# Attention units in a queue with wider distances, unnormalized head probabilities, gate b ahead of merge a, and no weight prefetch into the opening

## The chip, the cores and the metric

The kernel runs on one core of a Trainium2 chip. The metric is device time in microseconds, the median of several executions. One execution was also recorded by the hardware profiler; all views of the profile in this document are of that execution.

A core has TensorE (PE, matrix products from SBUF into PSUM), VectorE (DVE), ScalarE (ACT), GpSimd (POOL) and SyncE (SP, which here issues nearly all DMAs). Each engine works through its own list of instructions in order and waits on semaphores for the others.

## The reference

Two layers of a bidirectional encoder over 512 tokens with 1024 channels, in float32:

```
for i in range(DEPTH):                                   # 2
    h = rmsnorm(x, norm_mix[i])
    qa, ka, va, glu_in, qc, kc, vc, gates = split(h @ w_in[i])
    ya = diff_attention(qa, ka, va, ...)                 # 4 heads of two softmaxes
    yb = conformer_conv(glu_in, ...)                     # GLU, 31 taps, layernorm, silu
    yc = neighbourhood_attention(qc, kc, vc, rpb[i])     # 8 heads, 8x16 windows
    ga, gb, gc = split(sigmoid(gates))
    x = x + (ga * (ya @ w_br_a[i]) + gb * (yb @ w_br_b[i]) + gc * (yc @ w_br_c[i])) @ w_o[i]
    h = rmsnorm(x, norm_ffn[i])
    x = x + (silu(h @ w_ffn_gate[i]) * (h @ w_ffn_up[i])) @ w_ffn_down[i]
    h = rmsnorm(x, norm_ple[i])
    x = x + sigmoid(h @ w_ple_gate[i]) * (p[i] @ w_ple_in[i])
return rmsnorm(x, norm_final)
```

In differential attention a head has two softmaxes over 512 keys, and its output passes through an rmsnorm of its own:

```
a = softmax(s)                               # s: two score maps of a head
a = a[:, :, 0] - lam * a[:, :, 1]
o = rmsnorm(a @ v, subln_g) * (1 - lam_init)
```

## The kernel before

Activations lie channels by tokens: eight tiles of 128 x 512. Every float32 operand is split into a float32r high part (ACT copy, `split`, line 125) and a low part (DVE subtraction, line 139), and a product takes three matmuls: high x high, high x low, low x high (`mm3`, lines 159 to 161). A weight block of 128 x 1024 is loaded by SP into `wr` (512 KB) and split into `wh` and `wl` by `weights`; these instructions get a priority 400 instructions ahead of their place in the program (`w_ahead`).

The order on PE is the program's own. On the other engines and DMA queues a planner sets the order at compile time: among the instructions that it holds to be ready it takes the one with the highest priority, by its own estimates of durations.

A *tick* is four chunks of a projection; a chunk is the three matmuls of one 128-channel piece. At every tick the generators in `live` that are due take their next step, so that attention steps are placed between chunks of projections. A `yield n` in a generator means n ticks later. A unit is started by `run(gen, delay)`, with a delay in ticks after its head's projections.

A layer goes through these stages:
1. *glu*: eight projections, gated into `z`, the input of the convolution.
2. *natten*: four head pairs. `natten_in` projects Q and K, scales them, and `stack` builds by DMA the operands of `scores`, which hold high and low parts in the two halves of the partitions. Four units a pair: two score tiles of 128 x 256, exponential and normalization on ACT (`scale`), then transposes, then the product with V. Units start 3, 4, 5 and 6 ticks after the projections; the steps lie 2 and 1 ticks apart.
3. *diff*: four heads. `rope` copies a projection, lets DMA turn it, and combines both on DVE; then `stack`. Four units a head, one for each 128 queries (`probs`: two score maps, two maxima, two exponentials with their sums, the first map scaled by its reciprocal sum on ACT, the second subtracted on DVE), started 4, 6, 8 and 10 ticks after the projections. The odd units go on: transposes 2 ticks later, the product with V 1 tick later, and after the second half the head's norm: statistics 1 tick later, the broadcast of the result 2 ticks later.
4. *gate c* (eight projections, one of them among the heads), a sigmoid over all of them, *branch c*, *merge a* (per block a projection, a sigmoid and a product), *gate b* (eight projections), *merge b*, *w_o*, then *ffn* and *ple*.

The depthwise convolution is DVE work in the background: 4 x 31 taps (line 142, `conv_z`). `background` issues a given number of them (`BG`) behind a named instruction; `conv`, which is started at block 1 of gate b, issues what is left, sums the four results, and after two ticks PE forms the mean (`mu`, line 465, tile `conv_tr`).

PSUM has eight banks: `mm` 3 for projections, `sc` 2 for scores, `tr` 2 for transposes and norms, `av` 1.

`opening` loads x, the parameters and the first four weight blocks in pieces, and warms PE up with `WARM` matmuls on zeros. `final` does the last block of ple in two halves and the last norm.

Of the kernel before, what the change touches and what calls it, by code (L numbers as in the profile page):

```python
# [20 lines left out]
P = 128  # L21
# [26 lines left out]
WARM = 14  # L48
NORM = (1, 1)
BG = dict(glu=4, natten=3, gatec=2, branchc=2, mergea=4, mergea2=3)  # L50
# [8 lines left out]
class Net:  # L59
    def __init__(self, nc, tc, a):  # L60
        self.nc, self.tc, self.a = nc, tc, a
        self.uid = 0
        self.phase = "pre"
        self.act_set = None
        self.act_now = []
        self.act_prev = []
        self.live = []
        self.units = []
        self.wait = []
        self.now = 0  # L70
        self.chunks = 0
        self.col = self.rb = None

    def run(self, gen, delay=0):

        e = [self.now + delay, gen, self.phase]
        self.live.append(e)
        if not delay:
            self.step(e)
        return e  # L80
# [67 lines left out]
    def weights(self, ap, n):  # L148
        with self.tc.high_priority(offset=self.w_ahead):
            raw = self.sb("wr", [P, 1024])  # L150
            hi = self.sb("wh", [P, 1024], F32R)
            lo = self.sb("wl", [P, 1024], F32R)
            self.nc.sync.dma_start(raw[:, :n], ap[:, :n])
            self.split(hi[:, :n], lo[:, :n], raw[:, :n])
        return hi, lo
# [21 lines left out]
    def norm(self, sq, n, waits, done, spread=True):  # L177
# [10 lines left out]
        nc.vector.tensor_scalar(ms, sm, 1.0 / n, EPS, ALU.mult, ALU.add)  # L188
# [26 lines left out]
    def operand(self, x, g, tag):  # L215

        h = self.sb(tag, [P, 2, 512], F32R)
# [22 lines left out]
    def build(self):  # L240
        nc, tc, a = self.nc, self.tc, self.a
        self.bufs = dict(wr=2, wh=3, wl=3, h=8, qk=4, kh=2, v=4, pt=2, y=5, z=5, x=8, t=8, rp=4,
                         e=4, a=3, r=4, ss=1, sm=8, rc=4, b=4, s=8)
        self.bg, self.norm_on, self.w_ahead = BG, NORM, 400
# [12 lines left out]
    def opening(self):  # L257
# [5 lines left out]
        xc = [self.sb("x", [P, 512]) for _ in range(KD)]  # L263
# [7 lines left out]
        blocks = []  # L271
        for m in range(4):
            src = a["w_in"][0, (OFF_GLU + (0 if m % 2 else CB)) // P + m // 2]
            blocks.append((src, self.sb("y", [P, 1024], F32R), self.sb("qk", [P, 1024], F32R),
# [4 lines left out]
        for k in range(KD):  # L279
# [5 lines left out]
            if k in pieces:  # L285
                c0, c1, tag = pieces[k]
                for src, wh, wl, _ in blocks:
                    raw = self.sb(tag, [P, c1 - c0])
# [13 lines left out]
            self.tick()  # L302
        return h
# [51 lines left out]
    def layer(self, i, h, xsrc, xs):  # L355
# [14 lines left out]
        acc = []  # L370
# [83 lines left out]
    def conv(self, cs, ys):  # L454
# [16 lines left out]
        def done(col, rb):  # L471
            for j, c in enumerate(cs):
# [6 lines left out]
                y = self.sb("y", [P, 2, 512], F32R)  # L479
# [39 lines left out]
    def natten_in(self, pr, st, ys):  # L519
# [5 lines left out]
        qk = []  # L525
        for off in (OFF_QC, OFF_KC):
            ps = self.proj(off + pr * P)
            t = self.sb("t", [P, 512])
            r = self.rb if off == OFF_KC else st["r8"]
            self.background(self.tt(t, ps, r, ALU.mult), self.bg["natten"])  # L530
            qk.append(self.stack(t, off == OFF_KC))
        box = {}
        ys.append(self.sb("y", [P, 2, 512], F32R))
        for n in range(4):
            self.run(self.natten_unit(pr, n // 2, n % 2, *qk, st, box, ys[pr]), 3 + n)

    def natten_v(self, g, st):
# [6 lines left out]
        vd = [self.sb("x", [P, 2, 256], F32R) for _ in range(2)]  # L544
# [6 lines left out]
    def natten_unit(self, pr, half, u, q, k, st, box, y):  # L551
# [5 lines left out]
        for t in range(2):  # L557
            qt = 2 * half + t
            sc = self.ps("sc", (P, NW))
            self.scores(sc, q, k, u, slice(qt * P, (qt + 1) * P),  # L560
# [16 lines left out]
            self.scale(e[:, own], m[:, 2:3], self.norm_on[0])  # L577
# [25 lines left out]
        yield 1  # L603
# [18 lines left out]
    def gate_c(self, acc, m):  # L622
        self.phase = "gatec"
        ps = self.proj(OFF_G + 2 * D + m * P)
        g = self.sb("x", [P, 512])
        self.background(self.tt(g, ps, self.rb, ALU.mult), self.bg["gatec"])
        acc.append(g)
# [8 lines left out]
    def merge_a(self, ys, acc):  # L636
        for m in range(KD):
            self.phase = "mergea"
            ps = self.proj(OFF_G + m * P)
# [6 lines left out]
            self.background(self.tt(acc[m], acc[m], g, ALU.add), self.bg["mergea2"])  # L646

    def gate_b(self, cs, ys):
        gs = []
        for m in range(KD):  # L650
            self.phase = "gateb"
            if m == 1:
                conv = self.run(self.conv(cs, ys))
            ps = self.proj(OFF_G + D + m * P)
            if m % 2 == 0:
                two = self.sb("v", [P, 2, 512])
            g = two[:, m % 2]
            self.tt(g, ps, self.rb, ALU.mult)
            self.act(g, g, AF.Sigmoid, table="sigmoid")
            gs.append(g)  # L660
        self.drain(conv)
        return gs

    def merge_b(self, ys, acc, gs):
        self.phase = "mergeb"
        out = []
        for m in range(KD):
# [4 lines left out]
            mg = self.sb("qk" if m < 4 else "v", [P, 2, 512], F32R)  # L672
# [4 lines left out]
    def stack(self, t, key):  # L677

        nat = self.sb("kh", [P, 512], F32R)
        self.act(nat, t, AF.Copy)
        low = t.bitcast(F32R)
        self.tt(low, t, nat.bitcast(F32), ALU.subtract)
        sts = []
        for own, far in ((nat, low), (low, nat))[:2 if key else 1]:
            if own is low or not key:
                st = self.sb("qk", [P, 2, 512], F32R)
                st = [st[:, u] for u in range(2)]  # L690
            else:
                st = [self.sb("x", [P, 512], F32R) for u in range(2)]
            for u in range(2):
                rs, rx = slice(64 * u, 64 * u + 64), slice(64 - 64 * u, 128 - 64 * u)
                self.nc.sync.dma_start(st[u][rs].bitcast(F32), own[rs].bitcast(F32))
                self.nc.sync.dma_start(st[u][rx].bitcast(F32), far[rs].bitcast(F32))
            sts.append(st)
        return sts if key else st

    def scores(self, out, q, k, u, qs, ks):  # L700
        for n, st in enumerate(k):
            self.nc.tensor.matmul(out, q[u][:, qs], st[u][:, ks], start=n == 0, stop=n == 1)  # L702

    def rope(self, ps, cr, sr, key):
        raw = self.sb("rp", [P, 512])
        self.act(raw, ps, AF.Copy, scale=1.0 if key else 0.125)
        rot = self.sb("rp", [P, 512])
        for b in range(4):
            o = b ^ 1
            self.nc.sync.dma_start(rot[32 * b:32 * b + 32], raw[32 * o:32 * o + 32])  # L710
        self.tt(raw, raw, cr, ALU.mult)
        self.tt(rot, rot, sr, ALU.mult)
        self.tt(raw, raw, rot, ALU.add)
        return self.stack(raw, key)

    def diff_in(self, head, st, ys):
# [8 lines left out]
        q = self.rope(self.proj(OFF_QA + head * P), *st["tabs"], False)  # L725
        k = self.rope(self.proj(OFF_KA + head * P), *st["tabs"], True)
        box = {}
        for qt in range(4):
            self.run(self.diff_unit(head, qt, q, k, st, box, ys), 4 + 2 * qt)
# [5 lines left out]
    def diff_unit(self, head, qt, q, k, st, box, ys):  # L735
# [3 lines left out]
        box[qt] = self.probs(q, k, qt)  # L739
        if t == 0:  # L740
            return
        yield 2
# [12 lines left out]
        yield 1  # L755
# [9 lines left out]
        if half == 0:  # L765
            return
        o = self.sb("t", [P, 512])
# [10 lines left out]
        yield from self.norm(sq, P, (1, 2), done, spread=False)  # L778

    def scale(self, t, s, on_act):  # L780
        if on_act:
            self.act(t, t, AF.Copy, scale=s)
        else:
            self.nc.vector.tensor_scalar(t, t, s, None, ALU.mult)

    def probs(self, q, k, qt):
# [5 lines left out]
        for u in range(2):  # L792
            sc = self.ps("sc")
            self.scores(sc, q, k, u, qs, slice(0, 512))
# [3 lines left out]
                     accum_out=m[:, 2 + u:3 + u])  # L798
            es.append(e)
        nc.vector.reciprocal(m[:, 4:6], m[:, 2:4])  # L800
        nc.vector.tensor_scalar(m[:, 6:7], m[:, 5:6], self.nlam[:, i:i + 1], None, ALU.mult)
        self.scale(es[0], m[:, 4:5], self.norm_on[1])
        self.stt(es[0], es[1], m[:, 6:7], es[0], ALU.mult, ALU.add)
        return es[0]

    def w_o(self, mg, xsrc):
        self.phase = "wo"
        xs, h, st = [], [], []
        for m in range(KD):
            xo = self.sb("x", [P, 512])  # L810
# [9 lines left out]
    def ffn(self, h, x):  # L820
# [3 lines left out]
        for half in range(2):  # L824
# [23 lines left out]
            for m in range(KD):  # L848
# [3 lines left out]
                if half:  # L852
                    hn.append(self.norm_chunk(m, x[m], self.par(i, "ple", m),
                                              "qk" if m < 4 else "v", st))
# [49 lines left out]
    def final(self, h, x, pairs, hn, most):  # L904
# [50 lines left out]
        def store(c, col, tiles):  # L955
            r = self.sb("qk", [P, 1024])
# [3 lines left out]

        pg = [self.ps("mm", (P, 256)), None]
# [8 lines left out]
        rest(pi[0], 0)  # L970
        lows = [turn("av", 0, 0), turn("tr", 0, 1)]
# [119 lines left out]
```

## Time and profile before

| | |
|---|---|
| Time, median of 3 runs | 1901.37 us (1900.05 to 1901.43) |
| The profiled execution's own time | 1901.63 us |
| Its span, first to last instruction | 1899.8 us |
| Mean granted TensorE clock | 0.989 |
| PE busy | 1850.4 us (97%), 8912 matmuls |
| DVE busy | 1190.5 us (63%) |
| ACT busy | 769.3 us (40%) |
| POOL busy | 29.3 us (2%) |
| Moved by DMA | 213.82 MB, 113 GB/s in the mean |

Busy time is the time in which an engine had an instruction under way. [...] Waits are named by the instruction that waited and by the one whose end released it. The granted clock is 1.00 at full speed and 0.50 at half.

### The profile page before, as it was taken

The numbers are of one execution on the slowest core, as the hardware profiler recorded it, in microseconds if no ns is written. First come the engines' busy times: TensorE is split into PE (matmuls) and PEld (weight loads), VectorE is DVE, ScalarE is ACT, GpSimd is POOL, SyncE is SP. The second block draws the span as 40 slices with busy tenths as digits, with TensorE's granted clock in tenths as the row PEclk, the third lists the DMA queues.
The fourth block names the chain that finished last, engine by engine and source line by source line (L and its number), as shares of the span: only waits on it lengthen the run. The fifth ranks groups of instructions, "written<-read, shape, count | busy, mean of one in ns | idle before, by whom it ended". The sixth has DMA issues, their size and how long they took to land.

```text
span 1899.8 us, 23913 instructions
## 1 busy us (share of the span) xinstructions
PE 1850.4 (97%) x8912; PEld 1551.0 (82%) x8912; DVE 1190.5 (63%) x1921; ACT 769.3 (40%) x1296; POOL 29.3 (2%) x88
## 2 busy tenths in 40 slices
PE   8999989999999999999999998999999999999998
PEld 6898777887888888888888987788788888888887
DVE  6777677996654434445767767679876443344454
ACT  5466555224432222223525665443344322222343
POOL 0000000000000000000000000000000000000000
PEclk9999999999999999999999999999999999999999
DMA  5566432331432232222436654323233222322222
GB/s 181 157 171 178 123 105 57 105 111 61 161 105 95 85 104 103 97 84 92 143 121 176 177 142 133 89 62 100 94 117 133 95 100 79 110 100 93 88 89 86
DMA packets 89940, 213.82 MB, mean 113 GB/s; under 512 B 12256, under 2 KB 29792, under 8 KB 89824
## 3 DMA queue, kind: packets, MB, share of 16 engines
q1 hardware_dynamic: 89392, 211.60, 35.3%
q8 instruction: 71, 1.16, 0.3%
q10 hardware_dynamic: 432, 0.69, 0.1%
q14 instruction: 45, 0.37, 0.1%
HBM read 176.59 MB, written 4.19 MB: 95 GB/s over the span
## 4 chain that ended last, share of the span: by engine, by line
PE 87%; DVE 6%; DMA 3%; ACT 2%; SPq 1%; issue 1%; DVEq 0%; POOL 0%; POOLq 0%; ACTq 0%
PE ffn_mm L161 13%; PE ffn_mm L159 13%; PE ffn_mm L160 13%; PE mergea_mm L160 2%; PE mergea_mm L159 2%; PE mergea_mm L161 2%; PE wo_mm L159 2%; PE wo_mm L161 2%; PE wo_mm L160 2%; PE ple_mm L159 2%; PE ple_mm L160 2%; PE ple_mm L161 1%; PE natten_mm L159 1%; PE natten_mm L161 1%; PE natten_mm L160 1%; PE diff_mm L160 1%
## 5 line engine op out<-in xcount | busy, mean ns | idle before, releaser
L125 ACT ACTIVATE ffn_wh<-ffn_wr 128x1024 fp32r<-128x1024 f32 (+1 forms) x152 | 144.2, 949 | 511.6 <-issue 350.3
L159 PE MATMUL ffn_mm<-wo_h,ffn_wh 128*128 128x512 f32 x704 | 274.2, 390 | 0.0
L161 PE MATMUL ffn_mm<-wo_h,ffn_wl 128*128 128x512 f32 x704 | 273.9, 389 | 0.0
L160 PE MATMUL ffn_mm<-wo_h,ffn_wh 128*128 128x512 f32 x704 | 273.9, 389 | 0.0
L139 DVE TENSOR_TENSOR ffn_wl<-ffn_wr,ffn_wh 128x1024 fp32r<-128x1024 f32 (+1 forms) x152 | 164.9, 1085 | 129.3 <-ACT ffn_wh L125 129.3
L142 DVE SCALAR_TENSOR_TENSOR conv_z<-glu_z,pre_par,conv_z 128x512 f32<-128x512 f32 x240 | 179.1, 746 | 2.5
L161 PEld LDWEIGHTS ffn_mm<-wo_h,ffn_wl 128*128 128x128 f32 x704 | 132.2, 188 | 27.6
L160 PEld LDWEIGHTS ffn_mm<-wo_h,ffn_wh 128*128 128x128 f32 x704 | 132.2, 188 | 27.4
L159 PEld LDWEIGHTS ffn_mm<-wo_h,ffn_wh 128*128 128x128 f32 x704 | 132.2, 188 | 27.1
L139 DVE TENSOR_TENSOR ffn_t<-ffn_t,ffn_mm 128x512 f32<-128x512 f32 x44 | 30.2, 687 | 114.8 <-PE ffn_mm L161 114.8
L139 DVE TENSOR_TENSOR ffn_t<-ffn_mm,wo_r 128x512 f32<-128x512 f32 x44 | 30.4, 691 | 111.3 <-PE ffn_mm L161 111.3
L159 PE MATMUL ffn_mm<-ffn_z,ffn_wh 128*128 128x512 f32 x160 | 62.2, 389 | 0.0
L160 PE MATMUL ffn_mm<-ffn_z,ffn_wh 128*128 128x512 f32 x160 | 62.2, 389 | 0.0
L161 PE MATMUL ffn_mm<-ffn_z,ffn_wl 128*128 128x512 f32 x160 | 62.2, 389 | 0.0
L159 PE MATMUL ffn_mm<-ffn_y,ffn_wh 128*128 128x512 f32 x160 | 62.2, 389 | 0.0
L160 PE MATMUL ffn_mm<-ffn_y,ffn_wh 128*128 128x512 f32 x160 | 62.2, 389 | 0.0
L161 PE MATMUL ffn_mm<-ffn_y,ffn_wl 128*128 128x512 f32 x160 | 62.2, 389 | 0.0
L125 ACT ACTIVATE mergea_wh<-mergea_wr 128x1024 fp32r<-128x1024 f32 (+1 forms) x32 | 27.1, 848 | 82.8 <-PE mergea_mm L160 66.7
L795 DVE TENSOR_REDUCE diff_s<-diff_sc 128x1 f32<-128x512 f32 x64 | 42.3, 682 | 8.5 <-PE diff_sc L702 8.5
L125 ACT ACTIVATE natten_wh<-natten_wr 128x1024 fp32r<-128x1024 f32 x24 | 25.4, 1058 | 50.5 <-PE glu_mm L160 20.0
L139 DVE TENSOR_TENSOR wo_x<-wo_x,ffn_mm 128x512 f32<-128x512 f32 x32 | 22.0, 687 | 34.1 <-PE ffn_mm L161 34.1
L125 ACT ACTIVATE natten_e<-natten_b,natten_s 128x256 f32<-128x256 f32 x64 | 32.2, 503 | 27.1 <-DVE natten_s L565 25.8
(452 smaller groups left out, 4738.5 us busy)
## 6 DMA issues: line engine op xcount, KB each, us to landing
ffn_wr<-w_fg SPq DMA_DIRECT2D x44, 512.0 KB, 3.3
ffn_wr<-w_fu SPq DMA_DIRECT2D x44, 512.0 KB, 3.2
ffn_wr<-w_fd SPq DMA_DIRECT2D x32, 512.0 KB, 3.5
natten_wr<-w_in SPq DMA_DIRECT2D x16, 512.0 KB, 3.6
natten_b<-bias SPq DMA_DIRECT2D x64, 128.0 KB, 2.5
diff_wr<-w_in SPq DMA_DIRECT2D x16, 512.0 KB, 3.6
gatec_wr<-w_in SPq DMA_DIRECT2D x16, 512.0 KB, 3.7
mergea_wr<-w_in SPq DMA_DIRECT2D x16, 512.0 KB, 3.3
```

Of the source, the lines that this page charges most:

```text
L125: i = self.nc.scalar.activation(out, in_, func, **kw)
L139: return self.nc.vector.tensor_tensor(out, a, b, op)
L142: return self.nc.vector.scalar_tensor_tensor(out, a, s, b, op0, op1)
L159: mm(out, wh, ah, start=first, stop=False)
L160: mm(out, wh, al, start=False, stop=False)
L161: mm(out, wl, ah, start=False, stop=last)
L795: nc.vector.tensor_reduce(out=m[:, u:u + 1], in_=sc, op=ALU.max, axis=AX.X, negate=True)
```

## The change

- `opening`: `WARM` goes from 14 to 10. The priority of a weight block reaches back at most to the opening's end (`p0`), so no block of a later stage stands ahead of the opening's own loads. Its buffers are allocated in pairs.
- Units are put into a queue (`later`) with a delay and a gap: at each tick at most one unit starts, not before its delay is over and not before the gap behind the last one. natten: delay 5, gap 1; diff: delay 6, gap 2. The steps of a natten unit lie 2 and 2 ticks apart (2 and 1 before), those of a diff unit 3 and 2 (2 and 1 before).
- The first map of a diff head is left unnormalized. With s0 and s1 the sums of the exponentials e0 and e1, the unit forms e0 - lam (s0 / s1) e1, which is s0 times the row as it was. The head's norm takes the factor out, with its epsilon multiplied by s0 squared. ACT's copy of 128 x 512 per unit goes away.
- Gate b's first two blocks stand ahead of the sigmoids over gate c, its other six behind branch c and ahead of merge a. `conv` starts at block 4 of merge a. `BG` is set anew.
- Tiles of the tags `qk`, `x` and `v` are allocated as pairs of twice the size, half as many (`qk` 2 instead of 4, `x` 4 instead of 8); Q and K of a head or pair share one `qk` tile. The convolution's results move from `y` to `qk`, five merged blocks from `qk` and `v` to `y`.
- `final`: the sums of squares of the first seven blocks (`total(0, ...)`) move from the middle of the gate's products to behind the first half's products.

```diff
-WARM = 14
-NORM = (1, 1)
-BG = dict(glu=4, natten=3, gatec=2, branchc=2, mergea=4, mergea2=3)
+WARM = 10
+BG = dict(glu=4, natten=3, diff=1, gatec=2, branchc=1, gateb=4, mergea=3, mergea2=2)
...
     def tick(self):
         self.now += 1
         for e in list(self.live):
             while e in self.live and e[0] <= self.now:
                 self.step(e)
+        if self.queue and max(self.free, self.queue[0][0]) <= self.now:
+            _, gen, ph, gap = self.queue.pop(0)
+            self.free = self.now + gap
+            old, self.phase = self.phase, ph
+            self.run(gen)
+            self.phase = old
+
+    def later(self, gen, delay, gap):
+        self.queue.append((self.now + delay, gen, self.phase, gap))
...
+    def parts_of(self, tag, shape, n, dt=F32):
+        t = self.sb(tag, [P, n, *shape], dt)
+        return [t[:, k] for k in range(n)]
...
     def weights(self, ap, n):
-        with self.tc.high_priority(offset=self.w_ahead):
+        with self.tc.high_priority(offset=min(self.w_ahead, self.tc.cur_priority - self.p0)):
...
-    def norm(self, sq, n, waits, done, spread=True):
+    def norm(self, sq, n, waits, done, spread=True, eps=None):
...
-        nc.vector.tensor_scalar(ms, sm, 1.0 / n, EPS, ALU.mult, ALU.add)
+        if eps is None:
+            nc.vector.tensor_scalar(ms, sm, 1.0 / n, EPS, ALU.mult, ALU.add)
+        else:
+            self.stt(ms, sm, 1.0 / n, eps, ALU.mult, ALU.add)
...
     # layer()
         for m in range(1, KD):
             self.gate_c(acc, m)
-        for g in acc:
+        for m in range(2):
+            self.gate_b(gb, m)
+        for g in acc + gb:
             self.act(g, g, AF.Sigmoid, table="sigmoid")
         self.branch_c(acc, yc)
-        self.merge_a(ya, acc)
-        gb = self.gate_b(cs, yb)
+        for m in range(2, KD):
+            self.gate_b(gb, m)
+            self.act(gb[m], gb[m], AF.Sigmoid, table="sigmoid")
+        self.merge_a(ya, acc, cs, yb)
...
     # natten_in()
         for n in range(4):
-            self.run(self.natten_unit(pr, n // 2, n % 2, *qk, st, box, ys[pr]), 3 + n)
+            self.later(self.natten_unit(pr, n // 2, n % 2, st4, k2, st, box, ys[pr]), 5, 1)
...
     # natten_unit()
-        yield 1
+        yield 2
...
     # merge_a()
+            if m == 4:
+                conv = self.run(self.conv(cs, yb))
...
     # gate_b()
-            if m == 1:
-                conv = self.run(self.conv(cs, ys))
+        self.background(self.tt(gs[m], ps, self.rb, ALU.mult), self.bg["gateb"])
...
     # diff_in()
+            self.background(self.tt(raw, raw, st["tabs"][0], ALU.mult), self.bg["diff"])
...
+        box = dict(s0=self.sb("sm", [P, 4]))
         for qt in range(4):
-            self.run(self.diff_unit(head, qt, q, k, st, box, ys), 4 + 2 * qt)
+            self.later(self.diff_unit(head, qt, st4, k2, st, box, ys), 6, 2)
...
     # diff_unit()
-        yield 2
+        yield 3
...
-        yield 1
+        yield 2
...
+        eps = self.sb("sm", [P, 4])
+        self.stt(eps, box["s0"], EPS, box["s0"], ALU.mult, ALU.mult)
...
     # probs()
             self.act(e, sc, AF.Exp, table="exp", bias=m[:, u:u + 1],
-                     accum_out=m[:, 2 + u:3 + u])
+                     accum_out=m[:, 3:4] if u else s0[:, qt:qt + 1])
...
-        nc.vector.reciprocal(m[:, 4:6], m[:, 2:4])
-        nc.vector.tensor_scalar(m[:, 6:7], m[:, 5:6], self.nlam[:, i:i + 1], None, ALU.mult)
-        self.scale(es[0], m[:, 4:5], self.norm_on[1])
-        self.stt(es[0], es[1], m[:, 6:7], es[0], ALU.mult, ALU.add)
+        nc.vector.reciprocal(m[:, 4:5], m[:, 3:4])
+        self.stt(m[:, 5:6], m[:, 4:5], self.nlam[:, i:i + 1], s0[:, qt:qt + 1],
+                 ALU.mult, ALU.mult)
+        self.stt(es[0], es[1], m[:, 5:6], es[0], ALU.mult, ALU.add)
...
     # final()
-        products(pg[0], wg, h, 0, range(4))
-        total(0, most, range(4))
-        part = self.sb("sm", [P, 4])
-        nc.vector.tensor_scalar(part, sums[:, 0, :], 1.0 / D, EPS, ALU.mult, ALU.add)
-        products(pg[0], wg, h, 0, range(4, 8))
+        products(pg[0], wg, h, 0, range(8))
         gate(pg[0], 0)
         pi = [self.ps("sc", (P, 256)), None]
         products(pi[0], wi, pairs, 0, range(2))
         rest(pi[0], 0)
+        total(0, most, range(4))
+        part = self.sb("sm", [P, 4])
+        nc.vector.tensor_scalar(part, sums[:, 0, :], 1.0 / D, EPS, ALU.mult, ALU.add)
```

More of the change, by code (lines that the diff above doesn't have):

```diff
@@ L67, in __init__ @@
         self.live = []
-        self.units = []
+        self.queue = []
+        self.free = 0
         self.wait = []
@@ L72, in __init__, with run @@
         self.col = self.rb = None
-    def run(self, gen, delay=0):
-        e = [self.now + delay, gen, self.phase]
+    def run(self, gen):
+        e = [self.now, gen, self.phase]
         self.live.append(e)
-        if not delay:
-            self.step(e)
+        self.step(e)
         return e
@@ L262, in opening @@
         nc.scalar.dma_start(self.parts, a["par"])
-        xc = [self.sb("x", [P, 512]) for _ in range(KD)]
+        xc = [t for _ in range(KD // 2) for t in self.parts_of("x", [512], 2)]
         for k in range(2):
@@ L286, in opening @@
                 c0, c1, tag = pieces[k]
-                for src, wh, wl, _ in blocks:
-                    raw = self.sb(tag, [P, c1 - c0])
+                for m, (src, wh, wl, _) in enumerate(blocks):
+                    raw = raws[tag][m]
                     nc.sync.dma_start(raw, src[:, c0:c1])
@@ L534, in natten_in, with stack @@
         for n in range(4):
-            self.run(self.natten_unit(pr, n // 2, n % 2, *qk, st, box, ys[pr]), 3 + n)
+            self.later(self.natten_unit(pr, n // 2, n % 2, st4, k2, st, box, ys[pr]), 5, 1)
+    def stack(self, t, one, two):
+        nat = self.sb("kh", [P, 512], F32R)
+        low = t.bitcast(F32R)
+        self.split(nat, low, t)
+        for n, part in enumerate((nat, low)):
+            for st, r in ((one, 64 * n), (two, 64 - 64 * n)):
+                for u in range(2):
+                    if st is not None:
+                        self.nc.sync.dma_start(st[r:r + 64, u].bitcast(F32),
+                                               part[64 * u:64 * u + 64].bitcast(F32))
     def natten_v(self, g, st):
@@ L543, in natten_v @@
         edge = [vs[1][0:64, 0], vs[0][64:128, 1]]
-        vd = [self.sb("x", [P, 2, 256], F32R) for _ in range(2)]
+        vd = self.parts_of("x", [2, 256], 2, F32R)
         for n in range(2):
@@ L646, in merge_a, with gate_b @@
             self.background(self.tt(acc[m], acc[m], g, ALU.add), self.bg["mergea2"])
[L648 to L651, printed above, removed]
-            if m == 1:
-                conv = self.run(self.conv(cs, ys))
[L654 to L660, printed above, removed]
-        self.drain(conv)
-        return gs
+        self.drain(conv)
+    def gate_b(self, gs, m):
+        self.phase = "gateb"
+        ps = self.proj(OFF_G + D + m * P)
+        if m % 2 == 0:
+            gs += self.parts_of("v", [512], 2)
+        self.background(self.tt(gs[m], ps, self.rb, ALU.mult), self.bg["gateb"])
     def merge_b(self, ys, acc, gs):
@@ L675, in merge_b, with scores @@
         return out
[L677 to L714, printed above, removed]
+    def scores(self, out, st4, k2, u, qs, ks):
+        for n, st in enumerate((st4[:, 2 + u], k2[:, u])):
+            self.nc.tensor.matmul(out, st4[:, u, qs], st[:, ks], start=n == 0, stop=n == 1)
     def diff_in(self, head, st, ys):
@@ L776, in done, with probs @@
             ys.append(y)
[L778 to L786, printed above, removed]
+        yield from self.norm(sq, P, (1, 2), done, spread=False, eps=eps)
+    def probs(self, st4, k2, qt, s0):
         nc, i = self.nc, self.i
```

79 lines of the change are left out of this document (51 added, 28 removed).

## The prediction

> **What bounds the kernel now.** I read the page first, then who TensorE (PE) waited for over the whole span, then a table of windows by stage, then the timeline at the waits.
>
> ```profile
> PE 1850.4 (97%) x8912; PEld 1551.0 (82%) x8912; DVE 1190.5 (63%) x1921; ACT 769.3 (40%) x1296; POOL 29.3 (2%) x88
> ...
> PE   8999989999999999999999998999999999999998
> DVE  6777677996654434445767767679876443344454
> ```
>
> PE is the bound: a gain can come only from its idle time, and from time in which it runs slow. The waits name the idle time:
>
> ```profile
> PE conv_tr L465 <- DVE conv_ss L139: 6.7, 2, 3.4
> PE diff_tr L750 <- DVE diff_sm L186: 5.0, 2, 2.5
> PE diff_sc L702 <- DMA diff_x<-diff_rp: 4.3, 2, 2.3
> PE diff_sc L702 <- DMA diff_qk<-diff_kh: 4.3, 6, 1.4
> PE diff_tr L750 <- DVE diff_a L142: 3.4, 4, 1.3
> PE diff_sc L702 <- ACT diff_a L125: 3.2, 2, 1.6
> PE pre_mm L159 <- ACT pre_y L125: 2.9, 2, 2.5
> PE ple_tr L926 <- DVE ple_ss L139: 2.2, 1, 2.2
> ```
>
> Nearly every wait comes twice, once a layer. The windows (PE, PEld, DVE, ACT, POOL busy, then the granted clock) show where, and that the clock suffers there:
>
> ```profile
> 180.00:340.00 160.00, 148.06 (x762) 123.49 (x761) 114.81 (x201) 83.48 (x160) 5.01 (x7) 0.96 0.35 97
> 340.00:425.00 85.00, 85.00 (x377) 70.41 (x376) 84.09 (x120) 26.40 (x34) 0.00 (x0) 1.00 0.33 109
> 425.00:470.00 45.00, 41.64 (x179) 33.66 (x178) 29.47 (x46) 18.69 (x28) 1.01 (x1) 0.96 0.19 61
> ```
>
> 180 to 340 is differential attention: 11.9 us idle. 340 to 425 is branch c and merge a: PE full, but DVE full too (84.09 of 85), and its backlog is the 3.4 us that conv_tr waits just behind. What a wait does to the clock:
>
> ```profile
> 215.81 0.47 PE L702 MATMUL diff_sc<-diff_x,diff_qk 128*128 128x512 f32 x1 [2.04 <-DMA diff_x<-diff_rp]
> 217.63 0.77 PE L702 MATMUL diff_sc<-diff_qk,diff_qk 128*128 128x512 f32 x1 [1.36 <-DMA diff_qk<-diff_kh]
> ...
> 219.53 0.63 PE L159 MATMUL diff_mm<-glu_h,diff_wh 128*128 128x512 f32 x1
> 219.96 0.63 PE L160 MATMUL diff_mm<-glu_h,diff_wh 128*128 128x512 f32 x1
> ```
>
> Behind the two waits, matmuls start 0.43 us apart instead of 0.227. So I sized the loss from start-to-start distances in the timeline: whatever goes beyond the median of its form (0.227 us at 512 columns, 0.120 at 256, 0.109 for a transpose). It adds up to 74 us: 7.2 in the opening, 25.8 and 25.7 in the two layers' attention, 5.6 and 5.7 at conv_tr, 5.1 at the end (the rest rounding). That is all the change can win. The sum is made against the profiled execution, 1901.63 us (span 1899.8); the median of the runs is 1901.37, so they agree.
>
> **Opening.** Weight blocks of the stages behind it go first now:
>
> ```profile
> 0.74 0.86 SPq L153 DMA_DIRECT2D glu_wr<-w_in  x2
> 1.64 3.85 SPq L289 DMA_DIRECT2D glu_t<-w_in  x4
> ```
>
> Four such blocks (512 KB each) are read among the opening's 4.2 MB, at some 390 GB/s: about 5 us of transfer, and ACT and DVE split them (1.05 and 1.22 us each) ahead of the first operands. With the priority limited, parameters, x and the first pieces come first. Nearest row: a landing takes 2.2 us at least; from the issues at 0.7 to 1.6 that gives operands at about 4, split (0.72 + 0.40) by 5.5, instead of 9.10. Ten warm-up matmuls (eight at 0.43, the clock rising at 4.98 as now, two at 0.227) end at about 5.4, so the four removed are worth nothing alone. Gain 3.5 at the start; of the 2.8 us lost later in the opening I take 1 back, as x and w arrive earlier. **4.5 us**, between 1 (operands late, or the clock falling after the shorter warm-up) and 6. The next stage's weights now come behind the opening's 18 loads: landed by some 17 us, needed at 28; were that cover gone, one block costs 3.3 + 1.05 + 1.22 = 5.6.
>
> **Attention.** A tick is four chunks, 12 matmuls of 0.227 = 2.72 us. Counting ticks from the end of pair 0's K projection (T), differential heads are ready at T+24, 32, 38, 46; their units start now at +4, 6, 8, 10, later at +6, 8, 10, 12, but never two within two ticks. So:
> - First scores waiting for the stacked DMAs (1.26 in natten, 0.8 and 3.4 in diff): two ticks, 5.4 us, more. Gone.
> - Scores waiting for the exponentials (1.61 + 0.64 at T+42): there head 1's last and head 2's first unit share a tick and the two sc banks. Now two ticks apart. Gone.
> - Transposes waiting for diff_sm (2.5): the norm's statistics and the next unit's transposes share a tick and the tr banks. Later one tick lies between (statistics T+42, transposes 43, norm broadcast 44): 0.44 + 2.72 + 0.44 = 3.6 us against the 3.5 that the bank takes now. Gone or nearly; but the broadcast now waits for a bank whose split (197.38 to 201.46) takes 4.1 us: 0.5 to 1.5 us, three times.
> - Transposes waiting for diff_a (1.33 + 0.35): a tick more, and the chain is shorter by ACT's normalizing copy (0.72 us, 16 a layer; ACT is 40% busy, so this counts only in the chain). The scalar becomes one small SCALAR_TENSOR_TENSOR for TENSOR_SCALAR (0.21), and each head adds one for its epsilon: nothing.
> - The mid-natten wait (0.93 for natten_s) stays.
>
> That leaves per layer about 1.5 in natten, 3 at the broadcasts, and I take 2.5 for DVE being late: in 180 to 340 it has 114.8 us of work, later 8 taps of 0.75 more, in 160 less the 22 us lost there: 121 of 138. **7 instead of 25.7, 18.7 a layer, 37.5 in all**; between 3 (only the named rest) and 16 left.
>
> Buffers: the paired qk, x, y, v tiles hold as much as before. A head's stack needs the pair that the head two before frees with its last scores; those stand in PE's order at the end of this head's Q projection, and the stack's DMAs are issued about 5 us later. Cost nothing; otherwise SP waits, with the weight loads behind it. A natten unit takes its two bias loads along on SP (128 KB, 2.5 us to landing), later than the stacks and with idle room: in this stretch the DMA share is 0.35 to 0.62.
>
> **Gate b, convolution.** Eight gate b projections (43.5 us of PE) move ahead of merge a; their weight loads on SP, splits and sigmoids move along, in the order of their products; two blocks join gate c ahead of the sigmoids, so no table is loaded anew. Merge a before: 1.13 + 4 x 0.6 + 7 taps x 0.75 = 8.8 us of DVE steps a block in 8.16 of PE: the backlog. Later, blocks 0 to 3 have 5 taps: 7.3. But the taps now placed are 12 + 24 + 8 + 16 + 8 + 32 + 20 = 120 of 124, and the convolution's end starts inside merge a at block 4. Behind block 3's last add come 2 + 4 taps and a sum, some 6.4 us in series, up to 8.6 with what DVE does between, and conv_tr comes after two ticks, 5.4: it waits 1 to 3.2 us, I take 2, and 1 for the clock. From there the remaining convolution (now 448.7 to 460.8, 12 us beside an easy gate b) has five ticks, 13.6 us, beside merge a's 5.9 us of DVE: about 17, so merge b starts some 2 us late, between 0 and 4. **5 instead of 5.6**: 1.2 us won in both layers, between +7 and -7.
>
> **End.** The sums of squares move behind 18 more matmuls of 0.120 = 2.16 us. PE waits 2.24 there now, and the clock halves for 3.4 us right behind (0.88 mean from 1870). **2.7 us**, between 1 and 3.2.
>
> Sum: 4.5 + 37.5 + 1.2 + 2.7 = 45.9; 1901.6 - 45.9 = 1856.
>
> [...] In 180 to 340 the longest single wait is 2.5 us, and the clock is 0.96: 12.8 us at half speed, 6.4 us lost a layer. If short waits did not cause that, it would stay: 1856 + 13 = 1869. [...]
>
> **Rivals.**
> - DVE becomes the bound in attention and merge a (19%): 84.09 of 85 shows that it can. For: blocks 4 to 7 of merge a hold 33 us of DVE steps in 32.6 of PE. Against: the mean over 60 to 470, 320 us of 379, is 85%. Losses at their upper bounds (16 and 9 a layer): 1901.6 - 7.2 - 19.4 + 6.8 = 1882.
> - Opening unchanged, as the planner still finds SP free for the weight blocks first (5%): 1860.
> - Half clock stays (5%): 1869.
> - Slower (11%): the orders of ACT and DVE are fixed ahead of time. In 180 to 340 DVE stood 8.9 us before gatec_wl, because something ahead of it waited for PE's diff_tr and diff_sc; weight splits are queued behind such waits. With steps further apart, each unit step can hold the splits longer, and then PE waits for weights. 64 units lose 0.80 us each now (51.5 / 64). At 1.33 (the diff_a row) they lose 85: 1901.6 + 33.6 - 8.4 = 1927. It decides from 0.94 a unit. Against: no weight wait is among PE's rows.
>
> **Chances.** Forecast 58%, 1856, alone from 1843 to 1870; rivals as given; 2% for no change. A difference under 0.2% (3.8 us) can't be told. Faster 0.87, same 0.02, slower 0.11. The range: 1841 (all terms near their best; at their best 1840) to 1886 (the DVE case and a little beyond) leaves out the slower cases and the tails.
>
> **What would show it.** Right: no diff_sc wait for diff_x, diff_qk or diff_a; granted clock 1.00 in diff; first pre_mm before 6 us; ple_tr wait under 0.3; conv_tr wait 1 to 3. Wrong: PE waiting for wh or wl, or mm banks late by DVE in merge a; diff_tr waits moved to other releasers; half clock left in diff.

## The result and the profile after

The changed kernel takes 1853.15 us (median of 4 runs, 1851.95 to 1854.62), the kernel before 1900.94 (4 runs, 1900.05 to 1901.43): a ratio of 0.9749, with an interval of 0.9733 to 0.9766. The forecast was 1856, range 1841 to 1886. The profiled execution took 1853.27 us with a span of 1851.5.

The page of the changed kernel, busy time and PE's slices:

```profile
PE 1830.0 (99%) x8908; PEld 1541.9 (83%) x8908; DVE 1192.6 (64%) x1929; ACT 747.2 (40%) x1264; POOL 29.5 (2%) x88
...
PE   9999999999999999999999999999999999999998
```

PE's work is the same but for four warm-ups, and its busy time is 20 us lower all the same: matmuls at half clock count as longer ones (0.63 us for 128 x 512, 0.39 at full clock), and there are fewer of them: the mean granted clock is 0.996 instead of 0.989. The 8s of the opening's slice and of one slice in each layer's attention are gone. PE's waits after (total, times, longest):

```profile
PE conv_tr L492 <- DVE conv_ss L153: 7.4, 2, 3.7
PE natten_sc L717 <- DVE natten_s L607: 2.8, 1, 2.8
PE diff_sc L717 <- DMA diff_x<-diff_rp: 1.6, 1, 1.6
PE pre_av L287 <- DVE pre_zeror L357: 1.6, 1, 1.6
PE pre_mm L173 <- ACT pre_y L139: 0.9, 1, 0.9
PE diff_sc L717 <- DMA diff_rp<-diff_rp: 0.5, 1, 0.5
PE ple_sc L948 <- DVE ple_t L153: 0.4, 1, 0.4
```

The waits of differential attention have gone but for two ahead of first scores, 1.6 us in layer 0 and 0.5 in layer 1. The first row, at the convolution's mean, has grown, and the second is new as a wait of this size. The windows after, at the same stages (busy time of PE, PEld, DVE, ACT and POOL, then the granted clock, the DMA engines' share and GB/s):

```profile
178.00:337.00 159.00, 157.39 (x848) 134.88 (x847) 132.91 (x231) 78.60 (x155) 5.12 (x8) 1.00 0.38 111
337.00:424.00 87.00, 83.30 (x355) 67.78 (x354) 73.54 (x101) 26.51 (x36) 0.00 (x0) 0.96 0.27 90
```

Differential attention has 1.6 us of idle PE instead of 11.9, and the clock stays at 1.00. DVE is busy for 132.9 of 159 us there, with more taps beside it, and PE does not wait for it. The wait and the slow clock now lie in the second row.

A 128 x 512 matmul at full clock lasts 0.39 us in the records, and the next starts 0.227 us behind it. Measured as in the prediction, by what start-to-start distances exceed their usual values:

| us lost in | before | after | saved | saved as predicted |
|---|---|---|---|---|
| opening | 7.0 | 3.6 | 3.4 | 4.5 |
| attention, layer 0 | 25.8 | 7.5 | 18.3 | 18.7 |
| attention, layer 1 | 25.2 | 1.8 | 23.4 | 18.7 |
| merge a, gate b, convolution, both layers | 11.4 | 12.8 | -1.4 | 1.2 |
| end | 5.1 | 1.3 | 3.8 | 2.7 |
| all | 74.3 | 26.8 | 47.5 | 45.9 |

47.5 us saved here and four warm-ups at 0.227 make the 48.4 by which the two profiled executions differ. (Layer 1's attention comes out at 25.2 before, where the prediction had 25.7.) Nearly all of the attention's gain is differential attention's: it loses 2.7 and 1.5 us in the two layers instead of 21.9 and 22.3, while natten loses 4.9 and 0.4 instead of 4.0 and 3.1.

### The profile page after: what moved, and what is told of

It is laid out like the page before. It is cut to its first block, busy times and chain, and to the rows that moved or that the text cites. A ratio compares the mean times of both kernels' runs of the same rounds, so it can differ in the third digit from the quotient of the medians.

```text
span 1851.5 us, 23888 instructions
## 1 busy us (share of the span) xinstructions
PE 1830.0 (99%) x8908; PEld 1541.9 (83%) x8908; DVE 1192.6 (64%) x1929; ACT 747.2 (40%) x1264; POOL 29.5 (2%) x88
## 4 chain that ended last, share of the span: by engine, by line
PE 96%; DVE 2%; DMA 1%; issue 0%; ACT 0%; SPq 0%; POOLq 0%; DVEq 0%; POOL 0%; ACTq 0%
PE ffn_mm L173 13%; PE ffn_mm L174 13%; PE ffn_mm L175 13%; PE mergea_mm L173 2%; PE mergea_mm L174 2%; PE mergea_mm L175 2%; PE gatec_mm L174 2%; PE gatec_mm L175 2%; PE gatec_mm L173 2%; PE wo_mm L173 2%; PE gateb_mm L173 2%; PE gateb_mm L174 2%; PE gateb_mm L175 2%; PE wo_mm L174 2%; PE wo_mm L175 2%; PE ple_mm L174 2%
## 5 line engine op out<-in xcount | busy, mean ns | idle before, releaser
L139 ACT ACTIVATE mergea_wh<-mergea_wr 128x1024 fp32r<-128x1024 f32 (+1 forms) x32 | 27.1, 846 | 83.4 <-PE mergea_mm L174 52.4
L139 ACT ACTIVATE diff_a<-diff_sc,diff_s 128x512 f32<-128x512 f32 x32 | 22.0, 689 | 46.2 <-DVE diff_s L807 46.2
```

What stands on the lines that cost most here:

```text
L139: i = self.nc.scalar.activation(out, in_, func, **kw)
```

## The experiments: which part carries it

All kernels are the changed kernel but for the edit shown. The theory: the later starts (`later`) and the wider steps (`yield`) of the attention units carry the gain. By the expectations below, undoing both costs some 33 us, the starts alone 24 and the steps alone 6; opening and end carry 7; unnormalized probabilities and gate b's place carry nothing. No run separates the distances of natten from those of differential attention.

**e1: old starts and old steps.** (e2 is the part of the edit up to "4 + 2 * qt", e3 the three `yield` lines.)

```diff
-        self.queue.append((self.now + delay, gen, self.phase, gap))
+        self.live.append([self.now + delay, gen, self.phase])
-            self.later(self.natten_unit(...), 5, 1)
+            self.later(self.natten_unit(...), 3 + n, 1)
-            self.later(self.diff_unit(...), 6, 2)
+            self.later(self.diff_unit(...), 4 + 2 * qt, 2)
-        yield 2        # natten_unit, second step
+        yield 1
-        yield 3        # diff_unit, first step
+        yield 2
-        yield 2        # diff_unit, second step
+        yield 1
```

> The changed kernel with the units' old starts (natten 3 to 6, diff 4 to 10 ticks, no queue) and old steps (2 and 1 ticks); all else as changed. Theory (the distances carry the attention term): PE's excess in attention comes back to some 20 us a layer, less than the 25.7 of before only by what the shorter head chain saves; 1886 us (1878 to 1894). Rival (the shorter chain, the paired tiles and the new taps do it): under 1865.

1899.52 us (1896.0 to 1904.7), ratio 0.9993 (0.9983 to 1.0002): the whole gain is gone, 46.4 us. More than expected, since attention now loses 27.1 and 27.7 us, more than in the kernel before. PE's waits in this run's profile:

```profile
PE diff_sc L717 <- DMA diff_qk<-diff_rp: 7.2, 2, 3.6
PE diff_tr L764 <- DVE diff_a L156: 5.6, 2, 2.8
PE diff_tr L764 <- DVE diff_sm L200: 5.0, 2, 2.5
PE diff_sc L717 <- ACT diff_a L139: 3.2, 2, 1.6
```

The waits for diff_sm (2.5) and for the exponential (1.6) are those of before to the digit, and 3.6 for the stacks stands where two in a row made 3.4; the wait for diff_a has doubled, 2.8 instead of 1.33, though the chain to it is shorter by ACT's copy. So without the distances the rest of the change makes no difference that can be told: by the profile opening and end win 8 us, and attention gives 4 of them back; the rest lies within the 9 us by which the ten runs of this kernel spread. The paired tiles and the new taps, which this kernel keeps, bring nothing that can be told without the distances.

**e2: old starts, new steps.**

> Old starts, new steps (3 and 2 ticks in diff, 2 and 2 in natten). Theory, by the rows of before: first scores wait for the stacked DMAs again (1.9 in natten, 4.2 in diff), head 2's first unit for the exponentials (2.3), and the clock halves behind them (some 4): 12 us a layer, 1877 (1868 to 1885). Rival (the steps are what matters): under 1862.

1886.04 us (1885.2 to 1889.6), 0.9925 (0.9909 to 0.9942); attention loses 21.6 and 20.1. The scores stand ahead of their operands again:

```profile
PE diff_sc L717 <- DMA diff_qk<-diff_rp: 7.0, 3, 3.2
PE diff_sc L717 <- ACT diff_a L139: 6.1, 2, 3.1
```

The direction is the theory's; the size, 33 us over the changed kernel, exceeds the 24 expected and lies just outside the range. No wait for diff_sm is left, so that one goes with the steps.

**e3: new starts, old steps.**

> New starts with the queue, old steps. Theory: the transposes wait for diff_a (1.7 before, less the 0.7 of the dropped copy) and for the bank of the norm's broadcast, which shares their tick (0.9): 2 to 4 us a layer, 1859 (1855 to 1864). Rival (steps matter more than starts): over 1868.

1884.8 us (1884.2 to 1886.3), 0.9916 (0.9901 to 0.9931): a miss, the rival's side. The old steps cost 32 us over the changed kernel where 6 were expected. One wait carries it, with the half clock behind it (seven transposes in 1.76 us, where e1 has seven in 0.98). Here is its row in the list of waits, then DVE's timeline and PE's at its longest (the columns are start, duration, engine, line, operation, tile; in brackets the idle time before it and who ended it):

```profile
PE diff_tr L764 <- DVE diff_a L156: 19.5, 6, 4.4
```

```profile
227.83 0.69 DVE L153 TENSOR_TENSOR diff_rp<-diff_rp,diff_r 128x512 f32<-128x512 f32 x1
...
229.77 0.69 DVE L807 TENSOR_REDUCE diff_s<-diff_sc 128x1 f32<-128x512 f32 x1
...
235.35 0.74 DVE L156 SCALAR_TENSOR_TENSOR diff_a<-diff_e,diff_s,diff_a 128x512 f32<-128x512 f32 x1
```

```profile
236.15 1.76 PE L764 MATMUL diff_tr<-pre_ident,diff_a 128*128 128x128 f32 x7 [4.38 <-DVE diff_a L156]
```

The first score map was ready at about 223.9 (its matmuls start at 223.15 and 223.47), but DVE takes its maximum only at 229.77. Ahead of it in DVE's fixed list stand the rotations of the next head (`diff_rp`), which had themselves waited 3.29 us for their DMA at 222.90, two taps of the convolution and a weight split. The unit's result follows 5.6 us later, and the transposes, due at 231.77, wait 4.38. With the new steps no wait for diff_a is left. The tick more between scores and transposes is worth 2.72 us of that; the rest must come from DVE's order, which is planned anew with every change of the program, and which part is whose no run separates. The expectation took the price from a row of before (1.33), in which the scores came two ticks earlier and missed these rotations.

**The two distances are not additive.** Against e1, new steps alone win 13.5 us (e2), new starts alone 14.7 (e3), both 46.4. Each alone removes its own waits and lengthens others: new steps leave the first scores waiting for exponentials 6.1 us in total instead of 3.2, new starts leave the transposes waiting for diff_a 19.5 instead of 5.6.

**e7: the queue with its gap, but the old first delay** (3 and 4 ticks instead of 5 and 6; the new steps kept):

> The queue with its gaps (natten 1, diff 2 ticks) and the new steps, but the old first delays (3 and 4 ticks). It splits the starts into the gap between units and the delay to a head's first unit. Theory (the delay carries the starts' part, as first scores wait for the stacked DMAs): most of the 33 us of e2_old_starts stay lost, 1876 (1870 to 1884). Rival (no two units in a tick is what matters): 1862 or less.

1870.38 us (1867.8 to 1874.4), 0.984 (0.9825 to 0.9855), at the low end of the range, on neither side clearly. Of the 33 us between e2 and the changed kernel the gap brings 15.7, the delay the other 17.2; so the theory, which gave the delay most of it, had half. The diff_sc wait for diff_qk is left at 7.4 us in total (7.0 in e2), while the one for the exponential is gone: the gap keeps two units from sharing a tick, the delay lets the stacks land.

**e4: normalized probabilities, as before.** The norm's plain epsilon goes with it, and the first sum returns to `m[:, 2:3]`.

```diff
-        nc.vector.reciprocal(m[:, 4:5], m[:, 3:4])
-        self.stt(m[:, 5:6], m[:, 4:5], self.nlam[:, i:i + 1], s0[:, qt:qt + 1], ALU.mult, ALU.mult)
-        self.stt(es[0], es[1], m[:, 5:6], es[0], ALU.mult, ALU.add)
+        nc.vector.reciprocal(m[:, 4:6], m[:, 2:4])
+        nc.vector.tensor_scalar(m[:, 6:7], m[:, 5:6], self.nlam[:, i:i + 1], None, ALU.mult)
+        self.act(es[0], es[0], AF.Copy, scale=m[:, 4:5])
+        self.stt(es[0], es[1], m[:, 6:7], es[0], ALU.mult, ALU.add)
```

> The first map normalized on ACT again, the norm with its plain epsilon; all else as changed. Theory: with three ticks up to the transposes (8 us) the 0.72 us lie off the path; 1853 to 1856. Rival (the shorter chain carries part of the attention term): 1860 or more, with transposes waiting for diff_a.

1852.7 us (1851.5 to 1853.2), 0.9745 (0.9731 to 0.976): no difference. The 32 copies that ACT was spared are worth nothing that can be told at these distances.

**e5: gate b behind merge a, as before** (with the `BG` that belongs to it; its first two blocks also leave their place ahead of the sigmoids over gate c, and `merge_a` no longer starts `conv`).

```diff
-        for m in range(2, KD):
-            self.gate_b(gb, m)
-            self.act(gb[m], gb[m], AF.Sigmoid, table="sigmoid")
-        self.merge_a(ya, acc, cs, yb)
+        self.merge_a(ya, acc)
+        for m in range(KD):
+            if m == 1:
+                conv = self.run(self.conv(cs, yb))
+            self.gate_b(gb, m)
+            self.act(gb[m], gb[m], AF.Sigmoid, table="sigmoid")
+        self.drain(conv)
```

> Gate b behind merge a again, the convolution's end at its block 1, the taps set as before (none with diff and gate b, 4 and 3 in merge a); all else as changed. Theory: the place of gate b is worth nothing, as conv_tr waits 3.4 to 3.7 us in both places; 1853 (1850 to 1857). Rival (gate b's place carries part of the gain): 1858 or more.

1854.88 us (1853.6 to 1858.1), 0.9755 (0.9741 to 0.977): no difference that can be told. PE waits at conv_tr for 4.15 us a layer in the old order and 3.7 in the new. The old order waits although its `BG` places all 124 taps ahead of the convolution's end (12 + 24 + 16 + 16 + 56), four more than the new one: there the backlog that DVE carries out of merge a is enough. In the new order it is the taps left over (i1, below).

**e6: opening and end as before** (`WARM` 14, `offset=self.w_ahead`, `total(0, ...)` back in the middle of the gate's products).

> 14 warm-up matmuls, weight priority reaching into the opening, and the sums of squares in the middle of the gate's products, as before; all else as changed. Theory: the two ends are separate terms, 3.5 us at the opening and 3.7 at the end by the two traces; 1860 (1858 to 1862). Rival (the later stages take up what the opening loses): 1857.

1863.19 us (1861.6 to 1865.3), 0.9797 (0.9783 to 0.9812): both ends together carry 10.0 us, a little more than expected and just outside the range. The opening's excess is 6.8 again and the end's 5.0: 6.9 of the 10, and the four warm-ups are 0.9. Another 3.9 are in layer 0's attention, where the wait at natten_sc grew from 2.78 to 3.48 and the one at diff_sc from 1.6 to 2.0, and 1.6 less are lost in the convolutions, where the clock does not halve behind one of the two waits of 3.70 us (last section).

## The experiments: what is left

**i1: three taps instead of two behind each add of merge a**, `mergea2=3` in `BG`. The theory: conv_tr waits for a backlog of taps on DVE, so that four more of them placed earlier shorten it.

> One more tap behind each sum of merge a (mergea2 3 instead of 2), so that all 124 are placed ahead of the convolution's end and none is left over. Theory (the four left-over taps stand in series ahead of conv_tr): the wait falls from 3.7 to some 1.5 and the clock stays full, 4 to 5 us a layer; 1844 (1842 to 1848). Rival (DVE is full in merge a, the taps only move): 1852 or more.

1846.37 us (1845.0 to 1847.7), 0.9708 (0.9694 to 0.9722): as expected. The wait falls from 3.70 to 0.86 a layer, the clock does not halve behind it (in layer 0 matmuls start 0.23 us apart from 413.26), and the stage loses 1.5 instead of 6.9 and 5.9.

```profile
PE conv_tr L492 <- DVE conv_ss L153: 1.7, 2, 0.9
```

The 2.84 us less are about the four taps at 0.75. Attention loses 1.9 us more than in the changed kernel, so the medians differ by 6.8 us only, the profiled executions by 8.2.

**i2: the mean formed three ticks after the start of `conv` instead of two** (`yield 3` ahead of `mu`).

> The mean's matmul three ticks behind the sum instead of two. Theory: 2.7 us more cover leave a wait of 1, too short to halve the clock: 5 us a layer, 1843 (1841 to 1848). Rival (the convolution's end is then late for merge b, which waits in conv_tr's place): 1850 or more.

1852.28 us (1851.8 to 1854.1), 0.9741 (0.9724 to 0.9757): a miss.

```profile
PE mergea_mm L173 <- DVE mergea_t L153: 4.2, 2, 2.1
...
PE conv_tr L492 <- DVE conv_ss L153: 2.9, 2, 1.5
```

The wait at conv_tr falls to 1.46, but PE now waits 2.12 us a layer at `mergea_mm` for DVE's `mergea_t`, which stands behind the convolution's last steps: 3.58 us of waits instead of 3.70. A wait for a backlog moves when the waiting instruction does; it shrinks when the backlog does. The two waits of 1.46 and 2.12 us did leave the clock at full (0.998 in the mean over the run, 0.996 in the changed kernel), and the stage loses 4.5 us a layer instead of 6.4; attention and the opening took back 3 of it, 1.7 in the opening, where matmuls start 0.43 us apart up to 10.97 us.

**i3: `natten_v`'s eight copies issued by ACT instead of SP, on top of i1.**

```diff
-                    self.nc.sync.dma_start(v[o:o + 64, n].bitcast(F32), edge[n][:, part].bitcast(F32))
+                    self.nc.scalar.dma_start(v[o:o + 64, n].bitcast(F32), edge[n][:, part].bitcast(F32))
```

> As i1_taps, with the eight copies of natten's values (line 590) issued by ACT instead of SP. Theory (layer 0's wait of 2.8 to 3.0 us at natten_sc is for bias loads that SP could not issue ahead of these copies): the wait and its half clock go, some 5 us; 1841 (1839 to 1844). Rival (another cause): 1845 to 1848.

1856.07 us (1855.0 to 1857.2), 0.9762 (0.9745 to 0.9778): a miss, 9.7 us slower than i1. The natten_sc wait has gone, as the theory said, but ACT pays. Its timeline, and PE's behind it:

```profile
126.38 2.65 ACTq L590 DMA_DIRECT2D natten_x<-natten_v  x4
...
130.03 0.36 ACT L139 ACTIVATE natten_y<-natten_av 64x256 fp32r<-64x256 f32 x1
```

```profile
131.77 0.58 PE L173 MATMUL natten_av<-natten_pt,natten_v 128*128 128x256 f32 x1 [3.20 <-DVE natten_y L153]
```

Four issues hold ACT for 2.65 us, in 2.34 of which it computes nothing. Behind them it does a weight split, and only at 130.03 its part of freeing the single `av` bank; PE waits 3.20 us for that bank, 3.49 in layer 1.

**i4: i1, and the first pair's natten units one tick later** (`5 + (pr == 0)` for 5).

> As i1_taps, with the first pair's units a tick later (6 instead of 5). Theory: 2.7 us more cover leave some 0.3 of the wait at natten_sc, and the clock full; 1841 (1839 to 1844). Rival (the order that the planner gives SP's queue moves along with the units, and the wait stays): 1845 to 1848.

1841.14 us (1839.6 to 1841.9), 0.9683 (0.9669 to 0.9698): as expected. The natten_sc wait is gone, and layer 0's attention loses 5.3 us instead of 9.1 in i1. This is the fastest version: 12 us below the changed kernel, 60 below the one before.

**i5: i3, and the diff units one tick later** (`7, 2` for `6, 2`).

> As i3_copies_on_act, with the differential units' delay 7 instead of 6. Theory (the delay 6 is just short for head 2, whose first scores wait 1.6 us in layer 0 and 0.5 in layer 1): 2 us less than i3_copies_on_act, 1839. Rival (gate c's blocks then wait for the x buffers of the last head, or the planner's orders get worse): 1843 or more.

1851.53 us (1850.8 to 1853.1), 0.974 (0.9726 to 0.9755): 4.5 us faster than i3, where 2 were expected (the 1839 stood on a faster i3). No diff_sc wait is left; the waits that i3 brought stay (3.5 and 3.8 at natten_av).

## Why the prediction was right, and where its steps were off

**What bounds the kernel** held: PE does the same matmuls, and the saving is what left its idle time and its slow clock, 47.5 of 74.3 us. That the forecast lands within 3 us of the median is partly luck: its four terms are off by -1.1, +4.2, -2.6 and +1.1. Of its signs of being right, the granted clock in differential attention and the end of the ple_tr wait came; the first product before 6 us, conv_tr at 1 to 3 and no diff_sc wait for diff_x did not.

**Attention**: predicted 37.5, measured 41.7. The waits for the exponentials, for diff_sm and for diff_a have gone, those of the first scores for DMAs but for 1.6 and 0.5 us, and e1 to e3 and e7 show that the distances do it. The split of the gain between starts and steps, which the prediction's waits suggest, is wrong: it is no sum. The 3 us at the norm's broadcasts and the 2.5 for a late DVE did not appear, and the mid-natten wait of 0.93, which was to stay, went (layer 1 loses 1.8 in all). What did appear in layer 0 had been costed at nothing: the bias loads that move along with the natten units. SP's timeline of the changed kernel, and DVE's and PE's, in layer 0:

```profile
78.40 3.66 SPq L590 DMA_DIRECT2D natten_x<-natten_v  x6
82.17 0.52 SPq L605 DMA_DIRECT2D natten_b<-bias  x1
83.18 0.46 SPq L576 DMA_DIRECT2D natten_qk<-natten_kh  x1
...
86.11 2.54 SPq L605 DMA_DIRECT2D natten_b<-bias  x4
```

```profile
91.06 0.42 DVE L607 CUSTOM_DVE_ANT_0 natten_b<-natten_sc,natten_b 128x256 f32<-128x256 f32 x1 [0.49 <-DMA natten_b<-bias]
```

```profile
91.55 0.58 PE L717 MATMUL natten_sc<-natten_qk 128*128 128x256 f32 x1 [2.78 <-DVE natten_s L607]
...
92.15 0.63 PE L173 MATMUL natten_mm<-glu_h,natten_wh 128*128 128x512 f32 x1
92.57 0.63 PE L174 MATMUL natten_mm<-glu_h,natten_wh 128*128 128x512 f32 x1
```

A unit needs two bias tiles. Its first was issued at 82.17, its second only at 86.11, behind stacks and a weight load. Its scores stood ready at 85; DVE combined the second with its bias only at 91.06, and PE waited for the bank. In layer 1 SP spends the same 3.7 us on `natten_v`'s copies just before, but both tiles were issued together at 1001.25, and nothing waited: what differs is the second tile's place in SP's list. DVE's own idle time there is 0.49 us; before it a weight split stood in its list. i3 (SP relieved) and i4 (scores later) each remove this wait, but both also reorder DVE, so how much of the 2.78 us is the load's is not separated. "With idle room" was read from the DMA engines' share; the limit was SP's list of issues.

**Convolution**: predicted 1.2 saved, measured 1.4 lost. conv_tr waits 3.70, not 2. The chain was begun at block 3's last add, and the two ticks were counted from the end of that block on PE. But the add itself comes late. DVE's timeline of the changed kernel, then PE's:

```profile
404.81 0.69 DVE L153 TENSOR_TENSOR mergea_t<-mergea_t,mergea_mm 128x512 f32<-128x512 f32 x1
...
407.21 0.68 DVE L153 TENSOR_TENSOR gatec_x<-gatec_x,mergea_t 128x512 f32<-128x512 f32 x1
...
413.01 0.69 DVE L153 TENSOR_TENSOR conv_ss<-conv_ss,conv_z 128x512 f32<-128x512 f32 x1
```

```profile
413.84 2.04 PE L492 MATMUL conv_tr<-conv_ss,pre_ones 128*128 128x512 f32 x2 [3.70 <-DVE conv_ss L153]
```

From the block's product at 404.81 to the end of the sum are 8.9 us: product, a tap and a weight split (3.1 with the add), then the six taps, a split and the sum (5.8, where 6.4 was forecast: the chain was about right, its start was not). PE's two ticks were over at 410.14. Merge b, which the prediction had 2 us late, does not wait. So the term came out as 6.4 a layer instead of 5, 3.7 of it the wait and the rest the half clock, and i1 shows that in this order taps are its cause.

**Opening**: predicted 4.5, measured 3.4. The first product starts at 7.05 instead of 9.10, not at 5.5, so the estimate of the landing (about 4) was too early: 2.2 us is the shortest landing of `diff_qk` before, and here the loads of x issued in the first 10 us took 4.7 to 6.3; ACT's first split starts at 5.97, after 2.33 us of idle time that the DMA of x ends. The ten warm-ups ended at 6.17, not 5.4. Later weights came in time, and the clock did not fall (1.00 from 6.02 to 91.34); in i2's opening, with the same ten, matmuls start 0.43 us apart up to 10.97, a risk close to the one that the prediction named. **End**: predicted 2.7, measured 3.8; the ple_tr wait for ple_ss has gone, and the clock no longer halves there (1.00 from 1822 to 1849.2).

**The rivals.** DVE as the bound: it is at 84% in differential attention and PE does not wait for it; in merge a PE does, 3.7 us a layer at conv_tr, within the convolution's own term. Opening unchanged: fell, with the first product at 7.05. Half clock that stays: fell, the windows show 1.00 in differential attention. Slower, by splits queued behind waits: no weight wait appeared; but e3 shows a like mechanism, DVE's fixed order, with reductions behind rotations, at up to 4.4 us a wait, when only one of the distances is changed.

## What to carry to other kernels

Distances in a hand-placed order act together: here undoing one of two cost more than two thirds of what both won, so the value of each alone says little, and changing one alone can look like a failure. Read a moved step's DMAs against the issuing queue's own list, not against the DMA engines' share. A wait for a backlog is cured by earlier work (i1), not by a later reader (i2).

## What the runs showed of the hardware

The clock did not follow the length of a wait. In the changed kernel it halved behind 2.78 us (steps of 0.42 us from 92.15, above), in e1 behind 2.50 us at diff_sm (steps of 0.43 us from 266.63) and in i4 behind 1.98 us at diff_sc (128 x 256 matmuls 0.21 us apart from 212.44, instead of 0.12), but not behind 2.82 us at diff_a in e1 and not behind 1.61 in the changed kernel (1.00 from 178 to 337); in e6's opening it halved behind 1.70 and 0.55 (steps of 0.43 us from 11.04). PE's timeline of e1:

```profile
285.06 0.98 PE L764 MATMUL diff_tr<-pre_ident,diff_a 128*128 128x128 f32 x7 [2.82 <-DVE diff_a L156]
...
286.11 0.40 PE L717 MATMUL diff_sc<-diff_x,diff_qk 128*128 128x512 f32 x1
286.35 0.39 PE L717 MATMUL diff_sc<-diff_qk 128*128 128x512 f32 x1
```

The steps stay at 0.24 us. e6 has the plainest case: one instruction waits 3.70 us in each layer, and the clock halves in layer 1 alone.

```profile
421.78 1.10 PE L492 MATMUL conv_tr<-conv_ss,pre_ones 128*128 128x512 f32 x2 [3.70 <-DVE conv_ss L153]
...
1332.87 2.04 PE L492 MATMUL conv_tr<-conv_ss,pre_ones 128*128 128x512 f32 x2 [3.70 <-DVE conv_ss L153]
```

Two windows in which these waits end (PE's busy time, then the granted clock):

```profile
419.83:423.24 3.41, 1.46 (x5) 1.00 0.34 77
1331.19:1334.60 3.41, 1.73 (x3) 0.50 0.24 77
```

No run was made that shows why it halved behind the one and not behind the other. In the changed kernel it halved behind this wait in both layers (0.50 from 412.2 to 419.0 and from 1327.0 to 1330.4), and e6's convolutions lose 1.6 us less. So a difference of that size between two of these runs can come from the clock alone.
